# Two streams of matmuls on TensorE keep the order in which they are written; block sums one half product earlier, attention's stages at a higher priority

## The chip, the cores and the metric

The kernel runs on one core of one Trainium2 chip. The metric is the device time of one execution in microseconds (us); three runs of the kernel before gave a median of 1011.45 us. The engines are named as in the profile: PE is TensorE (matmuls), PEld its weight load, DVE is VectorE, ACT is ScalarE, POOL is GpSimd, and SP is SyncE, which issues all DMAs here.

## What is computed

One decoder layer on 256 tokens of width 2048, in fp32. All projections of `x` come first, then three branches (block attention, a gated spatial mix, attention into 256 memory tokens), each multiplied by a SiLU gate, projected to the model's width, weighted with a sigmoid gate, summed, projected once more and normalised:

```python
proj = x @ w_in
q_a, k_a, v_a, z_a, u_g, v_g, z_g, q_c, z_c, g_logit = split(proj)
y_a = _moba_attention(q_a, k_a, v_a) * silu(z_a)            # branch 0, 8 heads
y_g = _spatial_gating(u_g, v_g, w_s, b_s, ...) * silu(z_g)  # branch 1
mem_k, mem_v = mem @ w_mem_k, mem @ w_mem_v
y_c = _memory_attention(q_c, mem_k, mem_v) * silu(z_c)      # branch 2, 4 heads
gates = sigmoid(g_logit)                                    # (b, s, 3, d)
merged = (gates[:, :, 0] * (y_a @ w_branch_attn) + gates[:, :, 1] * (y_g @ w_branch_sgu)
          + gates[:, :, 2] * (y_c @ w_branch_mem))
x = _layer_norm(DN_ALPHA * x + merged @ w_out, ln_g, ln_b)
```

## The kernel before

Every fp32 product is made from fp32r parts. `split` (lines 58 to 60) copies a weight tile to its rounded part `hi` on ACT and computes the rest `lo = v - hi` on DVE; a product is then three matmuls (hi with x's hi, lo with x's hi, hi with x's lo). So each weight needs an ACT and a DVE operation ahead of its matmuls, and each of these matmuls has 512 columns or fewer.

After the memory projections two streams feed PE.

- **C, the classic stream** (`classic`, 160 half steps): the gates zc, then q of memory attention (qc), three gate tiles za, branch 2, five za, q and k of block attention, three ug, branch 0, five ug, zg with the spatial mix, branch 1. A half step of `channel_tile` is 16 matmuls on `acc` banks (`channels_mm`, lines 187 and 188); one of `gated_branch` is 12 (lines 712 to 714). Its weights come by SP as `raw` (line 122) and are split by `prep_half` into `hi`/`lo`, two half chunks ahead. There are three `acc` banks in PSUM; each step n of a `gated_branch` takes two of them (t = 0 and 1) and gives them back when DVE has multiplied them with the gate (`sg`, line 726).
- **S, the Strassen-like stream** (`s_stream`, 8 units of 7 block products, each in 2 halves: 112 half products of 12 matmuls, lines 386 to 388, tile `sM`). Unit u covers a block of weight columns (three branches' gate logits, v of two branches). `s_prep(s)` loads the x sums (`xf`) of half product s, subtracts weight blocks `b` in place on DVE (line 311: the one for the products M5, M6 and M4 ahead of the split, the one for M3 behind it), splits into `sh`/`sl`, and loads the next blocks (`s_load`). Half product s calls `s_prep(s + 2)` behind its matmuls; `sh` and `sl` share four buffers, so two half products are held at a time. `evacuate` copies or adds the results (k, lines 342 to 346), and `s_finish` stores them.

The driver (lines 775 to 783) emits one C half step, then as many S half products as keep S at 112 per 160 - LEAD - TAIL C steps, with LEAD, TAIL = 2, 14: the first S half products come after two C steps, and S ends 14 C steps before C does. `step` runs what the step before put in `late` (evacuations, stores), and `tick` advances each item in `pending` by one stage: an attention head has three (scores, transposes, values), whose result `put_y` splits into `yhl`, the branch's input.

This emission is not what the engines get. The tile framework's scheduler reorders instructions by its own model of times, taking among those that are ready the one with the best priority, by order of emission. Only what `tc.issue_after` ties stays in order. The instruction lists that each engine executes strictly in order are fixed at that point.

Of the kernel before, what the change touches and what calls it, by code (L numbers as in the profile page):

```python
# [1 line left out]

# [25 lines left out]
def decoder_layer(ctx, tc, xT, memT, x_tok, w_st, w_mv, w_mk, w_zc, w_qc, w_za, w_qk, w_ug, w_zg,  # L28
                  w_br, w_o, w_sT, sgu_bc, ln_g, ln_b, out):
    nc = tc.nc  # L30
# [11 lines left out]
    def w2(name, shape=(P, 512)):  # L42
        return work.tile(list(shape), F32, tag="w2", name=name, bufs=6)
# [27 lines left out]

    def tick():
        for item in list(pending):
            item.pop(0)()
            if not item:
                pending.remove(item)

# [107 lines left out]

    def channels_mm(ps, x, hi, lo, first, last):
        nc.tensor.matmul(ps, hi, x, start=first, stop=False)  # L187
        nc.tensor.matmul(ps[:, S:2 * S], lo, x[:, 0:S], start=False, stop=last)

    def channel_tile(xs, name, fin):  # L190

        ps = new_acc(name)
        for h in range(2):
            hi, lo = c_half()
            for k in range(8):
                c = slice(k * P, (k + 1) * P)
# [100 lines left out]

    B11, B12, B22, B21 = range(4)

    def s_prep(s):  # L300
        u, r = divmod(s, 14)
        if u >= UNITS:
            return
        p, h = divmod(r, 2)
        p = PRODUCTS[p]
        if p in FORM:
            t = wts.tile([P, 4, 2 * P], F32R, tag="xsf", name=f"xf{s}", bufs=3)
            nc.sync.dma_start(t.bitcast(F32), xf_d[FORM[p], h])
            xsf[s] = t
        b = lambda blk: rt[u, blk, h]  # L310
        sub = lambda o, x, y: nc.vector.tensor_tensor(o, x, y, op=ALU.subtract)  # L311
        src = {"M1": B11, "M5": B11, "M6": B11, "M4": B11, "M3": B22, "M7": B12, "M2": B21}[p]
        if p == "M5":
            sub(b(B11), b(B12), b(B11))
        elif p == "M6":
            sub(b(B11), b(B22), b(B11))
        elif p == "M4":
            sub(b(B11), b(B21), b(B11))
        hi = wts.tile([P, 2048], F32R, tag="shl", name=f"sh{s}", bufs=4)
        lo = wts.tile([P, 2048], F32R, tag="shl", name=f"sl{s}", bufs=4)  # L320
        split(hi, lo, b(src))
        shl[s] = (hi, lo)
        if p == "M3":
            sub(b(B12), b(B22), b(B12))
            s_load(u, B21, h)
        elif p == "M7":
            s_load(u + 1, B12, h)
        elif p == "M4":
            s_load(u + 1, B11, h)
        elif p == "M2":  # L330
            s_load(u + 1, B22, h)

    def snap(name):
        return work.tile([P, 512], F32, tag="snap", name=name, bufs=5)

    def s_stream(finish):

        bank, kept = {}, {}

        def keep(name, ps):  # L340
            kept[name] = snap(name)
            nc.scalar.activation(kept[name], ps, AF.Copy)

        def result(u, t, n, ps, name):
            r = kept[name]
            nc.vector.tensor_tensor(r, ps, r, op=ALU.add)
            finish(u, t, n, r)

        def evacuate(u, p):
            if p == "M1":  # L350
                keep(f"k1_{u}", bank["b"])
            elif p == "M5":
                keep(f"k5_{u}", bank["d"])
            elif p == "M6":
                keep(f"k6_{u}", bank["b"])
            elif p == "M3":
                result(u, 0, 1, bank["d"], f"k6_{u}")
            elif p == "M7":
                keep(f"k7_{u}", bank["b"])
                result(u, 1, 1, bank["b"], f"k5_{u}")  # L360
            elif p == "M4":
                result(u, 1, 0, bank["c"], f"k7_{u}")
            else:
                result(u, 0, 0, bank["a"], f"k1_{u}")

        BANK = {"M1": "b", "M6": "b", "M7": "b", "M5": "d", "M3": "d", "M4": "c", "M2": "a"}
        for s in range(14 * UNITS):
            u, r = divmod(s, 14)
            p, h = divmod(r, 2)
            p = PRODUCTS[p]  # L370
            if h == 0 and p in ("M1", "M5", "M4", "M2"):
                bank[BANK[p]] = new_sps(f"s{p}_{u}")
            ps = bank[BANK[p]]
            hi, lo = shl.pop(s)
            for kk in range(4):
                k = 4 * h + kk
                if p in FORM:
                    ah, al = xsf[s][:, kk, 0:P], xsf[s][:, kk, P:2 * P]
                else:
                    k += 0 if p == "M1" else 8  # L380
                    t = P if p == "M4" else 0
                    ah, al = xhl[:, k, t:t + P], xhl[:, k, S + t:S + t + P]
                c = slice(kk * 512, (kk + 1) * 512)
                first = h == 0 and kk == 0 and p in ("M1", "M5", "M4", "M2")
                last = h == 1 and kk == 3
                nc.tensor.matmul(ps, ah, hi[:, c], start=first, stop=False, skip_group_check=True)  # L386
                nc.tensor.matmul(ps, ah, lo[:, c], start=False, stop=False, skip_group_check=True)  # L387
                nc.tensor.matmul(ps, al, hi[:, c], start=False, stop=last, skip_group_check=True)  # L388
            xsf.pop(s, None)
            s_prep(s + 2)  # L390
            if h == 1:
                late.append(lambda u=u, p=p: evacuate(u, p))
            yield
# [303 lines left out]
    def gated_branch(b, order):  # L697
        for n in range(4):
            ps = [new_acc(f"b{b}_{n}{t}") for t in range(2)]
            g, prev = {}, {}  # L700
            for t in range(2):
                g[t] = w2(f"sg{b}{t}{n}")
                nc.sync.dma_start(g[t], gl_d[b, t, n])
                nc.scalar.activation(g[t], g[t], AF.Sigmoid)
            for half in range(4):
                hi, lo = c_half()
                for kk in range(2):
                    k = 2 * half + kk
                    c = slice(kk * 512, (kk + 1) * 512)
                    for t in range(2):  # L710
                        yh, yl = (yhl[b][:, k, o + t * P:o + (t + 1) * P] for o in (0, S))
                        nc.tensor.matmul(ps[t], yh, hi[:, c], start=(k == 0), stop=False)  # L712
                        nc.tensor.matmul(ps[t], yh, lo[:, c], start=False, stop=False)  # L713
                        nc.tensor.matmul(ps[t], yl, hi[:, c], start=False, stop=(k == 7))  # L714
                if half == 3:
                    late.append(lambda n=n, ps=ps, g=g: gated(b, order, n, ps, g))
                elif n == 0:
                    late.append(tick)
                yield
# [196 lines left out]
```

## Time and profile before

| | us |
|---|---|
| median of three runs (lowest, highest) | 1011.45 (1009.95, 1011.49) |
| the profiled execution | 1014.38 |
| its span in the profile | 1012.7 |
| PE busy | 982.4, 97% of the span |
| DVE busy | 820.6, 81% |
| ACT busy | 590.6, 58% |

The page's busy times say how full an engine is over the whole span. Where time can still be taken from PE is read in three other views: the stretches (busy time of each engine and TensorE's granted clock between two times), the list of waits (who ended PE's idle time), and the timelines of single instructions. A tile's name carries its number in the instruction lists below (`sh5_1211` is `sh` of half product 5), while the trace leaves numbers out.

### The profile page before, as it was taken

The page shows a single profiled execution, that of the slowest core. Times are in us where ns is not written, and L with a number is a line of the kernel's source. Part 1 is how long each engine was busy: PE and PEld are TensorE (multiplying, and loading weights), DVE is VectorE, ACT ScalarE, POOL GpSimd, SP SyncE. Part 2 cuts the span into 40 slices and gives each one's busy share as a digit, 9 for nine tenths or more (in the row PEclk, how much of TensorE's full clock was granted, in tenths as well). Part 3 has the DMA queues.
Part 4 walks back from the last instruction along what each step waited for, and adds up shares of the span by engine and source line. Part 5 has one row for each costly group of instructions (what it writes and reads, how often), then busy time and mean ns, then how long its engine had stood idle before and what let it go on. Part 6 is the DMA issues. An engine that isn't in the chain of part 4 may idle for free.

```text
span 1012.7 us, 12913 instructions
## 1 busy us (share of the span) xinstructions
PE 982.4 (97%) x4888; PEld 826.9 (82%) x4888; DVE 820.6 (81%) x800; ACT 590.6 (58%) x646; POOL 12.0 (1%) x17
## 2 busy tenths in 40 slices
PE   9999899999999999999999999979998999999995
PEld 7788788888888788888888888858877888878885
DVE  5865987898779799888979898899979877676657
ACT  5654665565577566556556566867555559554430
POOL 0000000000000000000000000000000010000000
PEclk9999999999999999999999999989999999999998
DMA  8899589738965897598379648937994785778622
GB/s 330 313 387 414 181 304 348 277 132 296 364 223 168 295 382 278 165 362 346 134 271 356 236 139 281 382 106 269 414 366 147 284 286 183 249 259 303 238 84 83
DMA packets 68126, 269.28 MB, mean 266 GB/s; under 512 B 7521, under 2 KB 21601, under 8 KB 45537
## 3 DMA queue, kind: packets, MB, share of 16 engines
q1 hardware_dynamic: 68064, 268.47, 72.2%
q8 instruction: 38, 0.62, 0.2%
q14 instruction: 24, 0.19, 0.0%
HBM read 245.37 MB, written 23.07 MB: 265 GB/s over the span
## 4 chain that ended last, share of the span: by engine, by line
PE 85%; DVE 5%; ACT 4%; DMA 3%; issue 2%; POOL 0%; SPq 0%; DVEq 0%; ACTq 0%
PE sM L386 9%; PE sM L387 9%; PE sM L388 9%; PE b L713 4%; PE b L714 3%; PE b L712 3%; PE zc L187 3%; PE k L187 3%; PE qc L187 3%; PE za L187 3%; PE q L187 3%; PE mk L187 3%; PE o L800 3%; PE o L799 3%; PE o L798 3%; PE mv L423 3%
## 5 line engine op out<-in xcount | busy, mean ns | idle before, releaser
L59 ACT ACTIVATE hi<-raw 128x1024 fp32r<-128x1024 f32 (+1 forms) x218 | 228.3, 1051 | 191.4 <-PE o L800 29.1
L60 DVE TENSOR_TENSOR lo<-raw,hi 128x1024 fp32r<-128x1024 f32 (+1 forms) x218 | 263.1, 1214 | 77.2 <-ACT hi L59 76.4
L60 DVE TENSOR_TENSOR sl<-b,sh 128x2048 fp32r<-128x2048 f32 x112 | 256.3, 2291 | 57.1 <-ACT sh L59 56.7
L59 ACT ACTIVATE sh<-b 128x2048 fp32r<-128x2048 f32 x112 | 214.4, 1915 | 99.6 <-PE sM L387 89.3
L311 DVE TENSOR_TENSOR b<-b,b 128x2048 f32<-128x2048 f32 x64 | 146.3, 2289 | 8.0 <-DMA b<-in_w_st_dram 7.8
L386 PE MATMUL sM<-sh,xf 128*128 128x512 f32 x256 | 101.3, 396 | 6.5 <-ACT sh L59 6.5
L387 PE MATMUL sM<-sl,xf 128*128 128x512 f32 x256 | 100.6, 393 | 2.5 <-DVE sl L60 2.5
L388 PE MATMUL sM<-sh,xf 128*128 128x512 f32 x256 | 100.2, 391 | 0.0
L387 PE MATMUL sM<-sl,xhl 128*128 128x512 f32 x192 | 76.8, 400 | 0.6 <-DVE sl L60 0.6
L386 PE MATMUL sM<-sh,xhl 128*128 128x512 f32 x192 | 77.4, 403 | 0.0
L713 PE MATMUL b<-lo,yhl 128*128 128x512 f32 x192 | 76.1, 397 | 1.2 <-DVE lo L60 1.2
L388 PE MATMUL sM<-sh,xhl 128*128 128x512 f32 x192 | 76.3, 397 | 0.0
L714 PE MATMUL b<-hi,yhl 128*128 128x512 f32 x192 | 74.9, 394 | 0.0
L712 PE MATMUL b<-hi,yhl 128*128 128x512 f32 x192 | 74.0, 398 | 0.9 <-ACT hi L59 0.9
L386 PEld LDWEIGHTS sM<-sh,xf 128*128 128x128 f32 x256 | 48.3, 189 | 18.3 <-ACT sh L59 7.9
L387 PEld LDWEIGHTS sM<-sl,xf 128*128 128x128 f32 x256 | 48.2, 188 | 12.9 <-DVE sl L60 3.2
L388 PEld LDWEIGHTS sM<-sh,xf 128*128 128x128 f32 x256 | 48.1, 188 | 10.3
L187 PE MATMUL ug<-xhl,hi 128*128 128x512 f32 x128 | 46.3, 400 | 1.5 <-ACT hi L59 1.5
L187 PE MATMUL q<-xhl,hi 128*128 128x512 f32 x128 | 46.5, 399 | 0.0
L187 PE MATMUL qc<-xhl,hi 128*128 128x512 f32 x128 | 46.2, 400 | 0.0
L187 PE MATMUL zc<-xhl,hi 128*128 128x512 f32 x128 | 45.7, 398 | 0.4 <-ACT hi L59 0.4
L187 PE MATMUL k<-xhl,hi 128*128 128x512 f32 x128 | 46.0, 397 | 0.0
(296 smaller groups left out, 1853.1 us busy)
## 6 DMA issues: line engine op xcount, KB each, us to landing
b<-in_w_st_dram SPq DMA_DIRECT2D x64, 1024.0 KB, 7.2
xf<-xf SPq DMA_DIRECT2D x64, 512.0 KB, 6.0
raw<-in_w_br_dram SPq DMA_DIRECT2D x24, 1024.0 KB, 6.8
raw<-in_w_qk_dram SPq DMA_DIRECT2D x16, 1024.0 KB, 7.3
raw<-in_w_o_dram SPq DMA_DIRECT2D x16, 1024.0 KB, 5.4
raw<-in_w_mk_dram SPq DMA_DIRECT2D x8, 1024.0 KB, 10.1
raw<-in_w_zc_dram SPq DMA_DIRECT2D x8, 1024.0 KB, 6.5
raw<-in_w_qc_dram SPq DMA_DIRECT2D x8, 1024.0 KB, 7.6
```

The costliest lines, as they stand in the source:

```text
L59: nc.scalar.activation(hi, v, AF.Copy)
L60: nc.vector.tensor_tensor(lo, v, hi.bitcast(F32), op=ALU.subtract)
L187: nc.tensor.matmul(ps, hi, x, start=first, stop=False)
L311: sub = lambda o, x, y: nc.vector.tensor_tensor(o, x, y, op=ALU.subtract)
L386: nc.tensor.matmul(ps, ah, hi[:, c], start=first, stop=False, skip_group_check=True)
L387: nc.tensor.matmul(ps, ah, lo[:, c], start=False, stop=False, skip_group_check=True)
L388: nc.tensor.matmul(ps, al, hi[:, c], start=False, stop=last, skip_group_check=True)
L423: nc.tensor.matmul(ps[t][n], lhs, rhs[:, n * 512:(n + 1) * 512], start=(k == 0 and rhs is hi and lhs is xh[t]), stop=(k == KT - 1 and lhs ...
L712: nc.tensor.matmul(ps[t], yh, hi[:, c], start=(k == 0), stop=False)
L713: nc.tensor.matmul(ps[t], yh, lo[:, c], start=False, stop=False)
L714: nc.tensor.matmul(ps[t], yl, hi[:, c], start=False, stop=(k == 7))
L798: nc.tensor.matmul(ps[:, 0:n], mh, hi, start=first, stop=False)
```

## The change

Four things are changed.

1. `in_turn` ties each piece of matmuls to the last matmul of the previous half step, whichever stream that was of: on PE, C half steps and S half products stay in the order in which the driver emits them. Inside an S half product or a gated half step the order stays free.
2. The block sums for M5, M6 and M4 leave `s_prep` for `s_sum`, which half product s calls as `s_sum(s + 3)` just ahead of `s_prep(s + 2)`: these 48 sums are emitted one half product before the split that reads them. The 16 for M3 stay in `s_prep`.
3. `tick` runs its stages under a higher priority for the scheduler.
4. LEAD, TAIL become 5, 11: S begins three C steps later and ends three later; the ratio stays 112 to 144.

```diff
+    behind = [None]
+    def in_turn():
+        return tc.issue_after(behind[0].ins) if behind[0] is not None else nullcontext()
@@ def tick():
-            item.pop(0)()
+            with tc.high_priority(100):
+                item.pop(0)()
@@ def channel_tile(xs, name, fin):
+            with in_turn():
+                for k in range(8):
+                    c = slice(k * P, (k + 1) * P)
+                    mm = channels_mm(ps, xs(8 * h + k), ...)
+            behind[0] = mm
@@
+    def s_sum(s):
+        u, r = divmod(s, 14)
+        if u >= UNITS:
+            return
+        p, h = divmod(r, 2)
+        other = {"M5": B12, "M6": B22, "M4": B21}.get(PRODUCTS[p])
+        if other is not None:
+            o = rt[u, B11, h]
+            nc.vector.tensor_tensor(o, rt[u, other, h], o, op=ALU.subtract)
@@ def s_prep(s):
-        if p == "M5":
-            sub(b(B11), b(B12), b(B11))
-        elif p == "M6":
-            sub(b(B11), b(B22), b(B11))
-        elif p == "M4":
-            sub(b(B11), b(B21), b(B11))
@@ s_stream: for s in range(14 * UNITS): for kk in range(4):
-                nc.tensor.matmul(ps, ah, hi[:, c], ...)      # and two more
+                with in_turn():
+                    nc.tensor.matmul(ps, ah, hi[:, c], ...)  # and two more, the last is mm
+            behind[0] = mm
             xsf.pop(s, None)
+            s_sum(s + 3)
             s_prep(s + 2)
@@ after the memory projections
     s_prep(1)
+    s_sum(2)
@@ gated_branch: for kk in range(2): for t in range(2):
+                        with in_turn():                      # the three matmuls, the last is mm
+                behind[0] = mm
@@
-    LEAD, TAIL = 2, 14
+    LEAD, TAIL = 5, 11
```

In the changed file the lines above move: `channels_mm` is at 194 and 195, the S matmuls at 401 to 403, the branch's at 731 to 733, the gate's multiplication at 746, the block sums at 318 (`s_sum`) and 331 (M3).

**Place 1, where the S stream begins.** On PE, around the end of gate tile zc0. Before:

```order
L187 MATMUL zc0_993<-xhl_96,hi16_1_890 128x512
L188 MATMUL zc0_993<-xhl_96,lo16_1_891 128x256
L386 MATMUL sM1_0_1063<-sh0_917,xhl_96 128x512
L387 MATMUL sM1_0_1063<-sl0_918,xhl_96 128x512
L388 MATMUL sM1_0_1063<-sh0_917,xhl_96 128x512
...
L386 MATMUL sM1_0_1063<-sh1_921,xhl_96 128x512
L386 MATMUL sM5_0_1154<-sh2_1079,xf2_1076 128x512
L387 MATMUL sM1_0_1063<-sl1_922,xhl_96 128x512
...
L187 MATMUL zc1_1037<-xhl_96,hi17_0_994 128x512
L386 MATMUL sM5_0_1154<-sh3_1121,xf3_1118 128x512
```

Half products 0, 1 and 2 of S (sh0 to sh2) stand between zc0 and zc1 here. After the change:

```order
L194 MATMUL zc0_994<-xhl_96,hi16_1_890 128x512
L195 MATMUL zc0_994<-xhl_96,lo16_1_891 128x256
L194 MATMUL zc1_1038<-xhl_96,hi17_0_995 128x512
L195 MATMUL zc1_1038<-xhl_96,lo17_0_996 128x256
...
L194 MATMUL zc1_1038<-xhl_96,hi17_1_1016 128x512
L195 MATMUL zc1_1038<-xhl_96,lo17_1_1017 128x256
...
L194 MATMUL zc2_1087<-xhl_96,hi18_0_1039 128x512
L195 MATMUL zc2_1087<-xhl_96,lo18_0_1040 128x256
...
L401 MATMUL sM1_0_1136<-sh0_917,xhl_96 128x512
L402 MATMUL sM1_0_1136<-sl0_918,xhl_96 128x512
```

Now zc1 and zc2 follow zc0, and half product 0 comes behind zc2. On DVE in the same stretch, before:

```order
L208 TENSOR_TENSOR zc0_1058<-zc0_993,zc0l_1059 128x256
L311 TENSOR_TENSOR b1_0_0_551<-b2_0_0_777,b1_0_0_551 128x2048
L60 TENSOR_TENSOR sl1_922<-b0_0_1_833,sh1_921 128x2048
L60 TENSOR_TENSOR sl2_1080<-b0_0_0_775,sh2_1079 128x2048
L311 TENSOR_TENSOR b0_0_1_833<-b1_0_1_608,b0_0_1_833 128x2048
L311 TENSOR_TENSOR b0_0_0_775<-b2_0_0_777,b0_0_0_775 128x2048
L60 TENSOR_TENSOR lo17_0_995<-raw17_841,hi17_0_994 128x1024
L60 TENSOR_TENSOR lo17_1_1016<-raw17_841,hi17_1_1015 128x1024
```

Here sl2 and two block sums stand between sl1 and lo17_0, the first `lo` of zc1. After the change:

```order
L217 TENSOR_TENSOR zc0_1059<-zc0_994,zc0l_1060 128x256
L331 TENSOR_TENSOR b1_0_0_551<-b2_0_0_777,b1_0_0_551 128x2048
L60 TENSOR_TENSOR sl1_922<-b0_0_1_833,sh1_921 128x2048
L318 TENSOR_TENSOR b0_0_1_833<-b1_0_1_608,b0_0_1_833 128x2048
L331 TENSOR_TENSOR b1_0_1_608<-b2_0_1_835,b1_0_1_608 128x2048
L60 TENSOR_TENSOR lo17_0_996<-raw17_841,hi17_0_995 128x1024
L60 TENSOR_TENSOR lo17_1_1017<-raw17_841,hi17_1_1016 128x1024
L60 TENSOR_TENSOR lo18_0_1040<-raw18_894,hi18_0_1039 128x1024
```

The split for half product 2 (sl2) and its next sum have left, and the sums of the second half (b0_0_1 and b1_0_1) stand ahead of lo17_0.

**Place 2, the step from n = 1 to n = 2 of branch 2.** On PE (b2_10 and b2_11 are the two banks of n = 1, b2_20 and b2_21 those of n = 2). Before:

```order
L712 MATMUL b2_10_2808<-hi38_1_2836,yhl2_1609 128x512
L712 MATMUL b2_11_2809<-hi38_1_2836,yhl2_1609 128x512
L712 MATMUL b2_20_2954<-hi39_0_2875,yhl2_1609 128x512
L387 MATMUL sM1_2_2673<-sl33_2803,xf33_2799 128x512
L388 MATMUL sM1_2_2673<-sh33_2802,xf33_2799 128x512
L386 MATMUL sM1_2_2673<-sh33_2802,xf33_2799 128x512
```

The matmuls of n = 1, of n = 2 and of half product 33 are mixed here. After the change:

```order
L732 MATMUL b2_11_2750<-lo38_1_2795,yhl2_1573 128x512
L733 MATMUL b2_11_2750<-hi38_1_2794,yhl2_1573 128x512
L731 MATMUL b2_20_2888<-hi39_0_2834,yhl2_1573 128x512
L732 MATMUL b2_20_2888<-lo39_0_2835,yhl2_1573 128x512
...
L731 MATMUL b2_21_2889<-hi39_0_2834,yhl2_1573 128x512
L732 MATMUL b2_21_2889<-lo39_0_2835,yhl2_1573 128x512
```

Now n = 2 starts right behind n = 1 without any of S between. On DVE, before:

```order
L60 TENSOR_TENSOR sl33_2803<-b0_2_1_2361,sh33_2802 128x2048
L60 TENSOR_TENSOR lo38_1_2837<-raw38_2698,hi38_1_2836 128x1024
L60 TENSOR_TENSOR lo39_0_2876<-raw39_2773,hi39_0_2875 128x1024
L60 TENSOR_TENSOR sl34_2869<-b2_2_0_2418,sh34_2868 128x2048
L60 TENSOR_TENSOR lo39_1_2913<-raw39_2773,hi39_1_2912 128x1024
L726 TENSOR_TENSOR sg201_2810<-b2_10_2808,sg201_2810 128x512
L60 TENSOR_TENSOR sl35_2906<-b2_2_1_2511,sh35_2905 128x2048
L726 TENSOR_TENSOR sg211_2813<-b2_11_2809,sg211_2813 128x512
```

Here sg201, which gives the first bank back, stands behind splits alone. After the change:

```order
L318 TENSOR_TENSOR b0_2_0_2399<-b2_2_0_2515,b0_2_0_2399 128x2048
L60 TENSOR_TENSOR lo39_0_2835<-raw39_2712,hi39_0_2834 128x1024
L318 TENSOR_TENSOR b0_2_1_2471<-b2_2_1_2594,b0_2_1_2471 128x2048
L60 TENSOR_TENSOR lo39_1_2869<-raw39_2712,hi39_1_2868 128x1024
L60 TENSOR_TENSOR sl32_2831<-b0_2_0_2399,sh32_2830 128x2048
L746 TENSOR_TENSOR sg201_2751<-b2_10_2749,sg201_2751 128x512
L746 TENSOR_TENSOR sg211_2754<-b2_11_2750,sg211_2754 128x512
```

Two block sums (L318), two `lo` and sl32 now stand directly ahead of sg201.

**Place 3, the end of n = 0 of branch 0, DVE.** The eighth attention head's result o7 becomes sza7 and then the last part of `yhl0`. Before:

```order
L608 TENSOR_TENSOR sza7_5203<-o7_5374,sza7_5203 128x256
L60 TENSOR_TENSOR sl85_5639<-b0_6_1_5462,sh85_5638 128x2048
L311 TENSOR_TENSOR b1_6_0_5292<-b2_6_0_5501,b1_6_0_5292 128x2048
L60 TENSOR_TENSOR sl86_5721<-b0_6_0_5425,sh86_5720 128x2048
L311 TENSOR_TENSOR b0_6_1_5462<-b1_6_1_5367,b0_6_1_5462 128x2048
L636 BN_STATS vst_5662<-vg_5405 128x6
L60 TENSOR_TENSOR yhl0_3644<-sza7_5203,yhl0_3644 128x256
L311 TENSOR_TENSOR b0_6_0_5425<-b2_6_0_5501,b0_6_0_5425 128x2048
L311 TENSOR_TENSOR b1_6_1_5367<-b2_6_1_5569,b1_6_1_5367 128x2048
L640 BN_AGGR vmv_5663<-vst_5662 128x2
L726 TENSOR_TENSOR sg000_5382<-b0_00_5380,sg000_5382 128x512
L726 TENSOR_TENSOR sg010_5385<-b0_01_5381,sg010_5385 128x512
```

Splits and sums of half products 85 and 86 stand between sza7 and yhl0 here, S being well ahead of the driver's order. After the change:

```order
L626 TENSOR_TENSOR sza7_5162<-o7_5332,sza7_5162 128x256
L60 TENSOR_TENSOR lo69_1_5441<-raw69_5288,hi69_1_5440 128x1024
L360 TENSOR_TENSOR k6_5_5362<-sM5_5_5116,k6_5_5362 128x512
L60 TENSOR_TENSOR sl79_5435<-b1_5_1_4631,sh79_5434 128x2048
L60 TENSOR_TENSOR yhl0_3575<-sza7_5162,yhl0_3575 128x256
L654 BN_STATS vst_5731<-vg_5459 128x6
L746 TENSOR_TENSOR sg000_5340<-b0_00_5338,sg000_5340 128x512
L746 TENSOR_TENSOR sg010_5343<-b0_01_5339,sg010_5343 128x512
```

Now lo69_1, the evacuation of half product 77 (into k6) and sl79 stand between them.

## Rows read from the trace of the kernel before

**Rows 1.** The page, engines: busy us, share of the span, instructions.

```profile
PE 982.4 (97%) x4888; PEld 826.9 (82%) x4888; DVE 820.6 (81%) x800; ACT 590.6 (58%) x646; POOL 12.0 (1%) x17
```

**Rows 2.** Stretches: start:end, length, busy us of five engines, TensorE clock, DMA share, GB/s.

```profile
100.00:125.00 25.00, 21.71 (x101) 17.54 (x100) 23.36 (x15) 14.83 (x14) 0.00 (x0) 0.93 0.58 201
400.00:500.00 100.00, 100.00 (x517) 84.80 (x516) 88.07 (x71) 60.00 (x66) 0.00 (x0) 1.00 0.70 256
650.00:700.00 50.00, 44.80 (x176) 35.16 (x175) 45.17 (x42) 37.54 (x40) 0.00 (x0) 0.90 0.55 203
740.00:790.00 50.00, 44.17 (x224) 36.35 (x223) 46.49 (x41) 29.14 (x30) 3.45 (x1) 1.00 0.63 232
```

**Rows 3.** Who PE waited for: us in total, times, longest.

```profile
PE sM L386 <- ACT sh L59: 6.5, 3, 2.8
PE sM L387 <- DVE sl L60: 3.1, 3, 1.8
PE mix L668 <- POOL ws L657: 1.8, 1, 1.8
```

**Rows 4.** Three stretches with a lower clock, columns as in rows 2.

```profile
106.30:112.40 6.10, 3.26 (x9) 2.49 (x9) 5.58 (x4) 4.82 (x5) 0.00 (x0) 0.72 0.48 187
667.70:672.20 4.50, 4.49 (x13) 3.57 (x14) 4.50 (x3) 2.20 (x3) 0.00 (x0) 0.62 0.00 0
679.00:685.80 6.80, 6.61 (x15) 4.86 (x16) 6.80 (x7) 1.50 (x3) 0.00 (x0) 0.51 0.00 0
```

**Rows 5.** Timeline of PE at the lower clock: start, us, line, tiles.

```profile
671.39 0.63 PE L387 MATMUL sM<-sl,xhl 128*128 128x512 f32 x1
671.82 0.50 PE L388 MATMUL sM<-sh,xhl 128*128 128x512 f32 x1
```

**Rows 6.** Timeline of PE where the S stream begins.

```profile
103.31 0.39 PE L386 MATMUL sM<-sh,xhl 128*128 128x512 f32 x1
103.54 0.39 PE L387 MATMUL sM<-sl,xhl 128*128 128x512 f32 x1
...
109.28 0.80 PE L386 MATMUL sM<-sh,xf 128*128 128x512 f32 x1 [2.84 <-ACT sh L59]
```

**Rows 7.** Timeline of ACT in the same stretch.

```profile
103.79 1.91 ACT L59 ACTIVATE sh<-b 128x2048 fp32r<-128x2048 f32 x1
...
107.02 0.42 ACT L491 ACTIVATE zc<-zc 128x256 f32<-128x256 f32 x1
...
109.14 1.99 ACT L59 ACTIVATE hi<-raw 128x1024 fp32r<-128x1024 f32 x2
```

**Rows 8.** Tile raw, issues from 98 to 104 us: durations, starts, landing.

```profile
L122 SPq DMA_DIRECT2D raw<-in_w_zc_dram x2: 333/356/378, 98.9 to 103.9; - x2
...
DMA to landing us min/median/max: 8.2/8.6/9.1
```

**Rows 9.** Timeline of DVE in the same stretch.

```profile
104.27 2.28 DVE L311 TENSOR_TENSOR b<-b,b 128x2048 f32<-128x2048 f32 x1
106.47 2.28 DVE L60 TENSOR_TENSOR sl<-b,sh 128x2048 fp32r<-128x2048 f32 x1
...
115.88 2.36 DVE L60 TENSOR_TENSOR lo<-raw,hi 128x1024 fp32r<-128x1024 f32 x2
```

**Rows 10.** Timeline of DVE, two short operations.

```profile
661.88 0.69 DVE L346 TENSOR_TENSOR k<-sM,k 128x512 f32<-128x512 f32 x1
...
674.42 0.41 DVE L60 TENSOR_TENSOR yhl<-sza,yhl 128x256 fp32r<-128x256 f32 x1
```

**Rows 11.** The page, groups: count, busy, mean ns, idle before and releaser.

```profile
L311 DVE TENSOR_TENSOR b<-b,b 128x2048 f32<-128x2048 f32 x64 | 146.3, 2289 | 8.0 <-DMA b<-in_w_st_dram 7.8
```

**Rows 12.** Tile ptT: count, ns least/median/most, first and last start.

```profile
L599 ACT ACTIVATE ptT<-pt x8: 473/492/494, 477.4 to 659.5; 128x384 f32<-128x384 f32 x8
```

**Rows 13.** Timeline of SP's DMA issues near the end.

```profile
869.40 0.38 SPq L403 DMA_DIRECT2D gl<-k  x1
...
877.05 1.48 SPq L703 DMA_DIRECT2D sg<-gl  x2
```

More of the change, by code (lines that the diff above doesn't have):

```diff
@@ L1 @@
-from contextlib import ExitStack
+from contextlib import ExitStack, nullcontext
 import concourse.bass as bass
@@ L187, in channels_mm @@
         nc.tensor.matmul(ps, hi, x, start=first, stop=False)
-        nc.tensor.matmul(ps[:, S:2 * S], lo, x[:, 0:S], start=False, stop=last)
+        return nc.tensor.matmul(ps[:, S:2 * S], lo, x[:, 0:S], start=False, stop=last)
     def channel_tile(xs, name, fin):
@@ L194, in channel_tile @@
             hi, lo = c_half()
-            for k in range(8):
-                c = slice(k * P, (k + 1) * P)
-                channels_mm(ps, xs(8 * h + k), hi[:, c], lo[:, c], h == 0 and k == 0, h == 1 and k == 7)
+            with in_turn():
+                for k in range(8):
+                    c = slice(k * P, (k + 1) * P)
+                    mm = channels_mm(ps, xs(8 * h + k), hi[:, c], lo[:, c], h == 0 and k == 0, h == 1 and k == 7)
+            behind[0] = mm
             if h == 1:
@@ L385, in s_stream @@
                 last = h == 1 and kk == 3
-                nc.tensor.matmul(ps, ah, hi[:, c], start=first, stop=False, skip_group_check=True)
-                nc.tensor.matmul(ps, ah, lo[:, c], start=False, stop=False, skip_group_check=True)
-                nc.tensor.matmul(ps, al, hi[:, c], start=False, stop=last, skip_group_check=True)
+                with in_turn():
+                    nc.tensor.matmul(ps, ah, hi[:, c], start=first, stop=False, skip_group_check=True)
+                    nc.tensor.matmul(ps, ah, lo[:, c], start=False, stop=False, skip_group_check=True)
+                    mm = nc.tensor.matmul(ps, al, hi[:, c], start=False, stop=last, skip_group_check=True)
+            behind[0] = mm
             xsf.pop(s, None)
+            s_sum(s + 3)
             s_prep(s + 2)
@@ L711, in gated_branch @@
                         yh, yl = (yhl[b][:, k, o + t * P:o + (t + 1) * P] for o in (0, S))
-                        nc.tensor.matmul(ps[t], yh, hi[:, c], start=(k == 0), stop=False)
-                        nc.tensor.matmul(ps[t], yh, lo[:, c], start=False, stop=False)
-                        nc.tensor.matmul(ps[t], yl, hi[:, c], start=False, stop=(k == 7))
+                        with in_turn():
+                            nc.tensor.matmul(ps[t], yh, hi[:, c], start=(k == 0), stop=False)
+                            nc.tensor.matmul(ps[t], yh, lo[:, c], start=False, stop=False)
+                            mm = nc.tensor.matmul(ps[t], yl, hi[:, c], start=False, stop=(k == 7))
+                behind[0] = mm
                 if half == 3:
```

## Prediction

> **What bounds the kernel now.** I read the page's engine totals first: PE is busy for 982.4 us, 97% of the span, and DVE for 820.6 [rows 1], so the end is set by PE's matmuls and by what PE waits for. The stretches say where it waits [rows 2]: from 400 to 500 us PE has no idle time at all, with DVE at 88%; from 100 to 125 it idles 25.00 - 21.71 = 3.29 us, from 650 to 700 5.20, from 740 to 790 5.83, together 14.3 us. The list of waits says on whom [rows 3]: 6.5 us in three waits of S matmuls for `sh`, 3.1 in three for `sl`, 1.8 in one of the spatial mix for POOL. So it is S that waits for its own weights, and the instruction lists show why: between sza7 and yhl0 (place 3) DVE splits half products 85 and 86, where the changed list has 79. S ran in a burst, faster than ACT and DVE can split for it, and it let C's weights lie ready.
>
> A wait costs more than its idle time. An S matmul is listed at 0.39 us, yet the next starts 0.23 us after it [rows 6]: a pipeline that runs dry loses 0.39 - 0.23 = 0.16 us. The list counts seven [rows 3], and 14.3 - 11.4 = 2.9 us are left for smaller ones; I take ten, 1.6 us. And behind the longer waits TensorE was granted its lower level (1.2 GHz) for a while: after the wait of 2.84 us at 109.28 [rows 6] and in two later stretches the mean clock was 0.72, 0.62 and 0.51 [rows 4]. At a mean of 0.62 over 4.5 us, (1 - 0.62) / 0.5 x 4.5 = 3.4 us lay at half clock; the others give 3.4 and 6.7. There matmuls start 0.43 us apart [rows 5] instead of 0.23, a loss of 1 - 0.23 / 0.43 = 46% of that time: 1.6, 3.1 and, in the first stretch, of which the wait itself is a part, 1.5. That is 6.2 us. All losses before: 14.3 + 1.6 + 6.2 = **22.1 us**. I sum against the profiled execution, 1014.38 us with a span of 1012.7; it lies 2.93 above the median of 1011.45, and I take the same 2.93 off at the end.
>
> **The change part by part.** Matmuls, splits and sums are the same in number, so every term is a wait. `in_turn` ties PE to PE, whose list is in order anyway: nothing waits for the tie itself; it costs the scheduler's freedom to put ready work into a gap. The three stretches of before lose their cause (no bursts, the sum no longer in the chain from a freed buffer to `sl`): all of the 22.1 us is given back. Against it stand the places that the instruction lists of the changed kernel show.
>
> (1) Place 1. PE goes from zc0, whose end is where S begins today (103.31 [rows 6]), straight to zc1, which needs raw17. That chunk is issued at 98.9 and lands at most 9.1 us later, at 108.0 [rows 8]. ACT is free by then: the SiLU of zc0 ends at 107.02 + 0.42 = 107.44, and hi17_0 takes 1.99 / 2 = 1.00 us [rows 7], so it is there at 109.1. DVE is the last one. Block operations follow each other at 106.47 - 104.27 = 2.20 us [rows 9]; as today the first sum stands at 104.27 and sl1 at 106.47, then come the two new ones at 108.67 and 110.87, then lo17_0 at 113.07, which takes 2.36 us for two, some 1.14 for the first [rows 9]: 114.2. PE loses 114.2 - 103.31 - 0.23 = 10.7 us, all of it on the path, for half products 0 to 2 that filled this gap are now behind zc2. The lower clock behind it costs between 1.5 and 3.1 (above); after a wait four times the longest so far I take the upper end. **13.8 us** (12.2 to 13.8). What is late next: raw18 is issued by 103.9 [rows 8] and lands by 113, before its turn.
>
> (2) Place 2, and the eight transitions like it in three branches. The second bank of step n + 1 is the first one of step n, free when the latter's multiplication (sg201) has run. Between sg200 and sg201 the changed DVE list has seven block operations, four `lo` and the two multiplications: 7 x 2.20 + 4 x 1.14 + 2 x 0.61 = 21.2 us, the multiplication taken from another 512-column operation of DVE, 0.69 less 0.08 of overlap [rows 10]. PE has 96 matmuls and the first six of b2_20, 102 x 0.23 = 23.5. So DVE keeps up by 2.3 us unless it is in a block operation when it should begin; the wait is 0 to 2.2 us. Over nine transitions I take 2.5 us in all (0 to 6.6, a third of nine times 2.2). The trace has three `acc` banks and PE at 100.00 of 100 us between 400 and 500 [rows 2], but only the gates and block attention run there, the first ptT at 477.4 [rows 12]. The Trainium skill (Perfetto Trace Analysis, Optimizing Tensor Performance, Matmuls) says that independent groups should rotate through PSUM banks so that one's evacuation overlaps the next one's matmuls; by that rule alone, three banks rotating, this term would be 0 and the sum 2.5 us lower, which no row here decides.
>
> (3) Place 3. The last part of `yhl` waits on DVE for the evacuation of half product 77, so for its last matmul: then 0.61 (as k, 0.69 [rows 10]), sl79 2.20 and yhl 0.33 (0.41 less the overlap [rows 10]), 3.1 us in all, against ten matmuls that PE still has, 2.3. PE waits 0.8 us, or up to 3.0 with one block operation more ahead. I take 2.0, since lo69_1 and the signals between the engines come on top, and half of a lower clock's 3.1 (the wait of 1.8 for POOL [rows 3] left the clock of its stretch at 1.00 [rows 2], that of 2.84 [rows 6] didn't): **3.5 us** (0.8 to 6.1).
>
> (4) Attention's stages come earlier, and head 2's values stand right behind its transposes on PE. The copy ptT takes 0.49 us [rows 12] and has one `hi` of 1.00 ahead [rows 7]: 0.5 to 1.5, I take **1.3 us**.
>
> (5) S in step with C: from the release of its buffers half product s + 2 needs `sh` 1.91 [rows 7] and `sl` 2.20, with a `lo` 1.14, a sum 2.20 (2.289 with its overlap [rows 11]) and an evacuation 0.61 between, 8.06 us. PE has one half product and some two half steps of C, 36 x 0.23 = 8.3. That is even: 0 most of the time, as between 400 and 500 [rows 2], up to 0.9 where a second evacuation stands ahead. Around units 5 and 6, where the norm of v adds to DVE, I take four at 0.8: **3.2 us** (0 to 4.5).
>
> (6) LEAD, TAIL. S ends three half steps later, so the last gate logits are stored later, and branch 1's step n = 2 loads them. Today 877.05 - 869.40 = 7.65 us lie between store and load on SP [rows 13]; three half steps are 36 x 0.23 = 8.3 us. 0 if it fits, 7.65 if all of it shows; I take **0.5**, since it fits with 0.6 to spare.
>
> `high_priority` and `s_sum` issue nothing of their own, and no DMA is added; SP's loads are moved with their half products past stores that wait for evacuations, 0 as long as they land in 8.2 to 9.1 us [rows 8].
>
> Sum after: 13.8 + 2.5 + 3.5 + 1.3 + 3.2 + 0.5 = 24.8 us, against 22.1: +2.7. 1014.38 + 2.7 - 2.93 = 1014.15, **1014.2 us**. The bounds go far: the low ends give 12.2 + 0 + 0.8 + 0.5 + 0 + 0 = 13.5, 8.6 us faster, 1002.9; the high ones 13.8 + 6.6 + 6.1 + 1.5 + 4.5 + 7.65 = 40.2, but not all at once.
>
> **The rivals.** *The order is as good as it looks* (faster). One mechanism: DVE is not in a block operation when a bank or a `yhl` is due, so transitions, place 3 and S's steps show next to nothing, and only (1), (4) and 1 us remain: 16.1 us, 6.0 less than before, 1005.4. It decides once (2), (3), (5) and (6), 9.7 us in my sum, together stay under 22.1 - 2.0 - 15.1 = 5.0 us. For it: 100 us without idle time at DVE's 88% [rows 2]. Against it: that stretch has no branch step and no burst either.
>
> *A wash*: these four come to between 5.0 and 9.0 us, and the result lies within 2.0 us of 1011.45.
>
> *The tail shows* (slower): the store and load of (6) are not hidden and sit ahead of a branch's splits on ACT: 7.2 us more than I took, 1021.4.
>
> *Every transition waits* (slower): sg2n1 and its like come a whole block operation late nine times, 9 x 2.2 = 19.8 us in place of 2.5: +17.3, 1031.5. Against it: DVE has room in its 88% with the same splits and sums [rows 2]. The Trainium skill (Perfetto Trace Analysis, Optimization Strategy) states that one gap repeating on the engine that should be saturated can mean too little SBUF or PSUM for the next tile; by that rule the three `acc` banks would be this gap. No run so far shows it.
>
> That the change doesn't do what it says is out: the lists show C and S alternating.
>
> **How the numbers follow.** The forecast, slower by more than 0.2% (2.0 us, about what a measurement of this kernel can tell from no change) but under 1020: 0.36. The wash: 0.30. Faster: 0.26. The tail 0.04, the transitions 0.04. So faster 0.26, same 0.30, slower 0.44. The likeliest case alone spans 1013.5 to 1020. The range must take in most of the faster case and the tail: 1003.5 to 1021.5, leaving out the transitions and the edges of both sides.
>
> **What would show it.** In the changed profile: one PE wait of some 10 us near 104, put down to `lo` on DVE, with a lower clock behind it (without it the sum is wrong by 13.8 us, and the change is faster); no idle time left at 650 to 700 and 740 to 790 of the kind `sM` on `sh`; waits of branch matmuls at line 731 on the gate's multiplication, 0 to 2.2 us each; one at 733 on `yhl` of 1 to 3 us; small waits of line 402 on `sl`. The forecast is wrong if the waits of S on `sh` and `sl` stay at 9.6 us, or if (2) is zero nine times.

## The result and the profile after

The changed kernel takes 1017.95 us (median of four runs, 1016.46 to 1020.71) against 1011.47 (1009.95 to 1011.71): a ratio of 1.0071, 95% interval 1.0049 to 1.0092. It is slower by 6.5 us. The profiled execution took 1017.01 us with a span of 1015.3.

The page's engine line and the list of PE's waits answer to [rows 1] and [rows 3]. The page gives busy us, share of the span and instructions for each engine:

```profile
PE 979.2 (96%) x4888; PEld 824.2 (81%) x4888; DVE 819.7 (81%) x800; ACT 586.9 (58%) x642; POOL 17.3 (2%) x17
```

The list gives who PE waited for, us in total, times and the longest:

```profile
PE zc L194 <- ACT hi L59: 5.4, 1, 5.4
PE zc L195 <- DVE lo L60: 4.9, 1, 4.9
PE b L731 <- DVE sg L746: 4.3, 3, 1.8
PE b L733 <- DVE yhl L60: 2.6, 1, 2.6
PE b L731 <- ACT yhl L59: 1.8, 1, 1.8
...
PE o L622 <- ACT ptT L617: 1.1, 1, 1.1
...
PE sM L402 <- DVE sl L60: 0.9, 2, 0.5
```

No S matmul waits for `sh` any more, and those for `sl` come to 0.9 us in place of 3.1. But the chain of C has taken over: zc1 waits twice, 10.3 us together, branch matmuls wait 4.3 us for banks (sg), 4.4 us for `yhl`. The stretches of [rows 2] but the one from 400 to 500 (start:end, length, busy us of PE, PEld, DVE, ACT and POOL, granted clock, DMA share, GB/s), and one more with the lower clock at place 1:

```profile
100.00:125.00 25.00, 14.68 (x70) 12.06 (x69) 17.56 (x12) 10.28 (x11) 0.00 (x0) 0.80 0.58 210
650.00:700.00 50.00, 45.62 (x195) 37.06 (x194) 42.51 (x38) 37.45 (x37) 0.00 (x0) 0.97 0.96 363
740.00:790.00 50.00, 50.00 (x258) 42.17 (x257) 44.59 (x45) 31.85 (x33) 1.12 (x2) 1.00 0.96 382
107.70:117.90 10.20, 4.93 (x14) 3.85 (x15) 8.21 (x6) 2.31 (x3) 0.00 (x0) 0.50 0.26 81
```

From 740 to 790 PE is now full, where it idled 5.83 us. From 650 to 700 the idle time is 4.4 us in place of 5.2, of another kind, and from 100 to 125 it is 10.3 in place of 3.29; from 107.7, at the end of the first of the two waits, the clock was at half for 10.2 us.

Place 1, on the timelines of PE, ACT and DVE (start, us, line, tiles; idle time before and what ended it in brackets). They answer to [rows 6], [rows 7] and [rows 9]:

```profile
108.06 0.80 PE L194 MATMUL zc<-xhl,hi 128*128 128x512 f32 x1 [5.42 <-ACT hi L59]
113.76 0.58 PE L195 MATMUL zc<-xhl,lo 128*128 128x256 f32 x1 [4.91 <-DVE lo L60]
```

```profile
106.95 2.00 ACT L59 ACTIVATE hi<-raw 128x1024 fp32r<-128x1024 f32 x2 [0.36 <-DMA raw<-in_w_zc_dram]
```

```profile
107.95 2.29 DVE L318 TENSOR_TENSOR b<-b,b 128x2048 f32<-128x2048 f32 x1
110.28 2.29 DVE L331 TENSOR_TENSOR b<-b,b 128x2048 f32<-128x2048 f32 x1
112.49 3.49 DVE L60 TENSOR_TENSOR lo<-raw,hi 128x1024 fp32r<-128x1024 f32 x3
```

The first wait ends when raw17 has landed and ACT has made hi17_0 (the first of the two copies from 106.95); the second lasts until DVE has been through the two sums that stand ahead of lo17_0 (L318 at 107.95, L331 at 110.28) and through lo17_0 itself.

At the first transition of branch 2, DVE and then PE:

```profile
322.67 2.28 DVE L331 TENSOR_TENSOR b<-b,b 128x2048 f32<-128x2048 f32 x1
324.88 1.22 DVE L60 TENSOR_TENSOR lo<-raw,hi 128x1024 fp32r<-128x1024 f32 x1
326.01 1.28 DVE L746 TENSOR_TENSOR sg<-b,sg 128x512 f32<-128x512 f32 x2
```

```profile
326.75 0.50 PE L731 MATMUL b<-hi,yhl 128*128 128x512 f32 x1 [1.75 <-DVE sg L746]
```

DVE goes from an M3 sum (L331) to a `lo` to the gate's two multiplications (L746) without a gap, and reaches these at 326.01, when PE has been through its six matmuls on the third bank. The bank is free when the first of the two is done, and PE goes on at 326.75. At the next transition, DVE and then PE:

```profile
347.16 1.28 DVE L746 TENSOR_TENSOR sg<-b,sg 128x512 f32<-128x512 f32 x2
347.90 0.50 PE L731 MATMUL b<-hi,yhl 128*128 128x512 f32 x1 [1.82 <-DVE sg L746]
```

From one pair of multiplications to the next DVE takes 347.16 - 326.01 = 21.15 us. PE has 84 matmuls between the two places where it needs a bank, starts on them at 326.75 and stands still from 347.90 - 1.82 = 346.08: 19.3 us. The difference is the wait.

At place 3:

```profile
657.82 0.68 DVE L360 TENSOR_TENSOR k<-sM,k 128x512 f32<-128x512 f32 x1
658.42 2.28 DVE L60 TENSOR_TENSOR sl<-b,sh 128x2048 fp32r<-128x2048 f32 x1
660.62 0.41 DVE L60 TENSOR_TENSOR yhl<-sza,yhl 128x256 fp32r<-128x256 f32 x1
```

```profile
661.09 1.22 PE L733 MATMUL b<-hi,yhl 128*128 128x512 f32 x2 [2.62 <-DVE yhl L60]
```

Evacuation, sl79, `yhl`, and PE is released: the chain of the prediction, link by link.

To compare places I added up, over all matmul starts of PE, what each step to the next start takes beyond 0.2285, 0.118 and 0.109 us (the usual steps behind 512, 256 and 128 columns). This holds waits and lower clock together, in us, for two profiles of either kernel (the second ones come from the experiments):

| stretch | before, 1st | before, 2nd | after, 1st | after, 2nd |
|---|---|---|---|---|
| whole span | 46.4 | 45.5 | 49.0 | 54.6 |
| place 1 (100 to 133) | 5.5 | 6.1 | 13.3 | 13.2 |
| branch 2 (318 to 376) | 0.3 | -0.4 | 4.8 | 7.7 |
| place 3 (645 to 672) | 5.5 | 5.5 | 6.5 | 6.8 |
| rest of branch 0 (672 to 712) | 5.9 | 5.0 | 0.1 | 0.0 |
| 712 to 900 | 9.3 | 9.1 | 3.3 | 4.5 |

### The profile page after: what moved, and what is told of

Its sections match the earlier page's. It is cut to its first block, busy times and chain, and to the rows that moved or that the text cites. A ratio compares the mean times of both kernels' runs of the same rounds, so it can differ in the third digit from the quotient of the medians.

```text
span 1015.3 us, 12897 instructions
## 1 busy us (share of the span) xinstructions
PE 979.2 (96%) x4888; PEld 824.2 (81%) x4888; DVE 819.7 (81%) x800; ACT 586.9 (58%) x642; POOL 17.3 (2%) x17
## 4 chain that ended last, share of the span: by engine, by line
PE 81%; DVE 8%; DMA 5%; issue 3%; ACT 2%; SPq 0%; DVEq 0%; ACTq 0%
PE sM L401 9%; PE sM L402 9%; PE sM L403 9%; PE qc L194 3%; PE za L194 3%; PE q L194 3%; PE zg L194 3%; PE o L820 3%; PE o L819 3%; PE o L818 3%; PE k L194 3%; PE b L733 3%; PE zc L194 3%; PE b L731 3%; PE ug L194 3%
## 5 line engine op out<-in xcount | busy, mean ns | idle before, releaser
L318 DVE TENSOR_TENSOR b<-b,b 128x2048 f32<-128x2048 f32 x48 | 109.6, 2283 | 9.2 <-DMA b<-in_w_st_dram 9.0
L401 PE MATMUL sM<-sh,xhl 128*128 128x512 f32 x192 | 75.8, 395 | 0.0
L403 PE MATMUL sM<-sh,xhl 128*128 128x512 f32 x192 | 75.3, 392 | 0.0
L731 PEld LDWEIGHTS b<-hi,yhl 128*128 128x128 f32 x192 | 36.0, 188 | 15.5 <-DVE sg L746 6.0
L194 PE MATMUL zg<-xhl,hi 128*128 128x512 f32 x128 | 45.8, 397 | 0.0
```

What stands on the lines that cost most here:

```text
L318: nc.vector.tensor_tensor(o, rt[u, other, h], o, op=ALU.subtract)
L403: mm = nc.tensor.matmul(ps, al, hi[:, c], start=False, stop=last, skip_group_check=True)
```

## The experiments

My first theory was the prediction's: the tie (`in_turn`) makes both the gain (S no longer runs ahead) and the loss (place 1 above all), so that filling place 1 with half products gives its 13 us back. Its rivals: the time is paid elsewhere; the earlier sums, the priority or LEAD do the harm. Each ratio below is to the kernel before, run beside it, with its 95% interval.

**b_again** is the kernel before, unchanged.

> The kernel before, unchanged, to see how far one profile of it stands for its other executions. Theory (the execution that I summed against carried lower-clock time that the others don't have, so that taking 2.93 us off the changed kernel as well was wrong): ratio 1.000, and the new profile's execution lies within 1.5 us of the median of 1011.5, with less than 3 us lost at the lower clock behind the waits of 650 to 690 us, where I counted 4.7. Rival (every profiled execution is about 3 us longer than a plain one): the profile shows about 1014.4 us again.

Ratio 1.0008 (0.9996 to 1.0019). The profiled execution took 1013.53 us, 2.0 above the 1011.5 that I had named, and there was one stretch of 3.4 us less at the lower clock than in [rows 4]:

```profile
667.60:671.00 3.40, 3.04 (x7) 2.46 (x8) 3.40 (x2) 2.53 (x4) 0.00 (x0) 0.50 0.00 0
681.30:684.70 3.40, 3.40 (x10) 2.66 (x9) 3.40 (x3) 1.06 (x1) 0.00 (x0) 0.50 0.00 0
```

At 46% that is 6.8 x 0.46 = 3.1 us, a little over what I expected, so neither side was quite right. But 17 runs of the kernel before that were timed beside it go from 1010.05 to 1014.73 with a median of 1011.95: 1014.38 was an execution from the upper end, and 2.93 us were its own. Nor do other kernels show an offset of profiled executions: that of the changed kernel (1017.01) and that of no_turn (999.90) lie below their medians.

**no_turn** takes the tie out of the changed kernel:

```diff
 def in_turn():
-    return tc.issue_after(behind[0].ins) if behind[0] is not None else nullcontext()
+    return nullcontext()
```

> The changed kernel without the tie between C and S: the scheduler orders PE freely again; sums, priority and LEAD, TAIL as changed. Theory (the order on PE makes both the gain and the loss): PE starts as before with half products 0 to 2 behind zc0, place 1 costs under 4 us, S runs in bursts again and waits for sh and sl for over 6 us; 1008 to 1013 us. Rival (the earlier sums or the priority lengthen DVE's way to lo and sg, whatever the order on PE): 1016 to 1020.

1001.02 us, ratio 0.9895 (0.9881 to 0.9910): 11 us faster than before and 17 faster than the changed kernel, beyond what my theory allowed. Waits of PE:

```profile
PE sM L401 <- ACT sh L59: 3.1, 2, 2.8
PE sM L402 <- DVE sl L60: 2.4, 3, 1.8
```

So the tie alone costs 17 us. It does take away more of S's waits (0.9 us are left with it, 5.5 without, where I expected over 6, and 9.6 before), but the other parts of the change gain without it. By the measure of the table above, 8.0 of the 17 us lie at place 1, 4.1 in branch 2, 2.8 at place 3 and 2.2 from 712 to 900. The lists of DVE, ACT and SP change with the tie too, so this is its price together with what the scheduler then makes of them.

**lead2** sets LEAD, TAIL back in the changed kernel:

```diff
-    LEAD, TAIL = 5, 11
+    LEAD, TAIL = 2, 14
```

> The changed kernel with LEAD, TAIL = 2, 14 as before. Here half product 0 stands behind the first half step of zc1, but zc1 still follows zc0 directly on PE, and on DVE the same two block operations stand ahead of lo17_0. Theory (the tie makes place 1, not LEAD): the wait of some 10 us at zc1 stays; 1015 to 1019 us. Rival (place 1 comes from S beginning three C steps later): the wait falls under 4 us and the time to 1004 to 1008.

1022.34 us, ratio 1.0096 (1.0081 to 1.0112). The two waits of zc1 are there as before:

```profile
PE zc L194 <- ACT hi L59: 5.7, 1, 5.7
PE zc L195 <- DVE lo L60: 4.7, 1, 4.7
PE b L731 <- ACT yhl L59: 3.6, 1, 3.6
PE b L731 <- DVE sg L746: 3.6, 1, 3.6
PE mix L686 <- POOL ws L675: 2.8, 1, 2.8
```

Place 1 belongs to the tie, not to LEAD. The time lies above my 1015 to 1019. By the table's measure 12.2 us are lost behind 672 us, where the changed kernel loses 3.4: the wait of 3.6 for sg stands in branch 0 here, and the mix waits 2.8. Branch 2, without a wait for a bank, loses 3.8 less.

**lead_only** and **prio_only** are the kernel before with one part each:

```diff
-    LEAD, TAIL = 2, 14
+    LEAD, TAIL = 5, 11
```

> The kernel before with LEAD, TAIL = 5, 11 and nothing else. Theory (without the tie the gain of 11 us comes from S being emitted three C steps later: it then runs less far ahead, half product 80 instead of 84 beside o7 on PE): most of the gain, 1002 to 1006 us, the waits of sM on sh and sl near 650 to 700 and 740 to 760 fall from 9.6 us to under 6. Rival (the gain comes from attention's stages having priority): 1009 to 1013.

```diff
 for item in list(pending):
-    item.pop(0)()
+    with tc.high_priority(100):
+        item.pop(0)()
```

> The kernel before with the higher priority for the stages of tick and nothing else. Theory (LEAD makes the gain): 1008 to 1012 us. Rival (priority makes it, sza7 and yhl coming earlier, so that C has work and S stops running ahead; half product 81 instead of 84 beside o7 on PE): 1001 to 1006.

lead_only 1004.82 us, 0.9938 (0.9915 to 0.9960); prio_only 1009.80, 0.9974 (0.9963 to 0.9986). LEAD gives 6 to 7 us and the priority 2 to 3; together with the sums, in no_turn, it is 11. Waits of lead_only:

```profile
PE sM L386 <- ACT sh L59: 5.2, 3, 2.8
PE sM L387 <- DVE sl L60: 3.5, 2, 2.6
```

The detail of my theory for lead_only isn't borne out: its waits for `sh` and `sl` were to fall under 6 us and are 8.7 in this profile, whose execution (1010.94 us) was the slowest of its eight. In prio_only they come to 8.3. The time is settled, the way it is saved in this kernel isn't.

The fourth part needs no run. The instruction lists of all five engines are the same, in the same order, whether the 48 sums are emitted at their old place or one half product ahead, in the kernel before as in the changed one: `s_sum` moves nothing. The lists of no_turn are those of the kernel before with LEAD and priority alone.

With this the tie can be priced twice: prio_only to lead2 is +12.5 us, no_turn to the changed kernel +17.

**first3** fills place 1 in the changed kernel:

```diff
-    while done_s < S_STEPS and done_s * (C_STEPS - LEAD - TAIL) < (done_c - LEAD) * S_STEPS:
+    while done_s < S_STEPS and (done_s < 3 and done_c >= 2
+                                or done_s * (C_STEPS - LEAD - TAIL) < (done_c - LEAD) * S_STEPS):
```

> The changed kernel, but the driver emits half products 0, 1 and 2 right behind zc0, so that they stand between zc0 and zc1 on PE again, as before; all else stays. Theory (place 1 is lost on the path: 10.3 us of waiting and about 2.5 at the lower clock): the waits of zc1 for hi17_0 and lo17_0 fall from 10.3 us to under 2, and the time from 1017.95 by 11 to 13 us to 1005 to 1007, ratio to before 0.994 to 0.996. Rival (the gap at place 1 is slack that S pays for elsewhere: whoever starts S earlier waits for its blocks or for C later): under 4 us gained, 1014 or more.

1028.09 us, ratio 1.0155 (1.0137 to 1.0173): 10 us slower than the changed kernel, where I expected 11 to 13 faster. The theory fell, and the rival's mechanism came out larger than its own words:

```profile
PE b L731 <- DVE sg L746: 6.7, 3, 4.0
PE mix L686 <- POOL ws L675: 5.9, 1, 5.9
PE sM L402 <- DVE sl L60: 4.0, 2, 2.4
PE zc L195 <- DVE lo L60: 2.4, 4, 1.0
```

Place 1 did shrink: in place of 10.3 us PE waits 2.4 us for sl1 (at 108.69) and 2.4 for `lo`. But the lists of DVE, ACT and SP moved as well, far behind the place that was edited. A bank of branch 0 comes 4.0 us late at 703, and the mix now waits 5.9 us at 823 for POOL's select on `ws`, which took 9.71 us. The timeline of POOL, and the busy times meanwhile (columns as above):

```profile
813.04 9.71 POOL L675 TENSOR_SCALAR_AFFINE_SELECT ws<-ws 128x128 f32<-128x128 f32 x1 [19.16 <-DMA ws<-in_w_sT_dram]
```

```profile
813.00:823.00 10.00, 4.11 (x24) 3.33 (x23) 9.61 (x10) 3.46 (x3) 9.71 (x1) 0.80 0.26 76
```

**sums_behind** changes one thing in the changed kernel: each block sum is queued on DVE behind the last `lo` of C that was emitted before it, so that at place 1 lo17_0 follows sl1 directly.

```diff
 def split(hi, lo, v): ...
-    nc.vector.tensor_tensor(lo, v, hi.bitcast(F32), op=ALU.subtract)
+    return nc.vector.tensor_tensor(lo, v, hi.bitcast(F32), op=ALU.subtract)
@@ prep_half
-    split(hi[:, c:c + n], lo[:, c:c + n], ...)
+    lo_last[0] = split(hi[:, c:c + n], lo[:, c:c + n], ...)
@@ s_sum, and the M3 sum of s_prep
+    with tc.issue_after(lo_last[0].ins):
         nc.vector.tensor_tensor(o, rt[u, other, h], o, op=ALU.subtract)
```

> The changed kernel, with each block sum queued on DVE behind the last lo of C that was emitted before it: at place 1 lo17_0 now follows sl1 directly. Theory (4.9 us of place 1 are the two sums ahead of lo17_0): the wait of zc1 for hi17_0 stays at 5 to 6 us, the one for lo17_0 falls from 4.9 to about 1.1, and the time by 3 to 5 us to 1013 to 1015. Rival (as where S began earlier, the other lists move with it, and a tied PE can't step aside): no gain, 1016 to 1024.

1006.03 us, ratio 0.9934 (0.9916 to 0.9952): 12 us faster than the changed kernel, more than twice what I expected, and faster than the one before. Its waits, and DVE at place 1:

```profile
PE zc L194 <- ACT hi L59: 5.4, 1, 5.4
PE b L733 <- DVE sg L748: 4.5, 3, 2.5
PE sM L404 <- DVE sl L60: 2.4, 1, 2.4
...
PE zc L195 <- DVE lo L60: 0.5, 1, 0.5
```

```profile
106.21 2.29 DVE L60 TENSOR_TENSOR sl<-b,sh 128x2048 fp32r<-128x2048 f32 x1 [1.37 <-ACT sh L59]
109.33 2.36 DVE L60 TENSOR_TENSOR lo<-raw,hi 128x1024 fp32r<-128x1024 f32 x2 [0.83 <-ACT hi L59]
```

The first wait of zc1 stays at 5.4 us and the second falls from 4.9 to 0.5, as the theory says. The rest of the gain is at place 3: no wait for `yhl` is left there, and the stretch from 645 to 672 loses 1.5 us in place of 6.5. By the same measure place 1 loses 8.2 in place of 13.3; the two profiled executions differ by 9.8 us. In DVE's list `yhl` now stands ahead of lo69_1, the evacuation and sl79. The waits for sg stay (4.5 us).

**first3_behind** adds the half products of first3 to that:

> The changed kernel with both: the block sums behind C's splits, and half products 0 to 2 between zc0 and zc1. Theory (half products 0 to 2 cover the landing of raw17, which is the 5.4 us that is left at place 1, but half product 2 then waits some 2.5 to 3 us for sh2 and sl2, as in the kernel before): the wait for hi17_0 falls from 5.4 to under 1, the gain against the sums alone (1006.0) is 2 to 4 us, 1002 to 1004, with no mix wait over 2 us. Rival (starting S early is what hurts the later stages, by the mix for POOL and sg at 703): 1008 to 1016, with these waits back.

1004.44 us, ratio 0.9923 (0.9904 to 0.9942):

```profile
PE sM L404 <- DVE sl L60: 4.5, 3, 2.4
PE b L733 <- DVE sg L748: 2.0, 3, 0.8
...
PE zc L195 <- DVE lo L60: 1.5, 3, 1.1
```

The wait for hi17_0 is gone, no mix wait is left, and the span of the profile is 5.6 us shorter than that of sums_behind. The time lies just above my 1002 to 1004. In the times the gain of 1.6 us is within what two intervals overlap, so it isn't established. It does show that starting S early was not what hurt first3; the lists that came with it were.

**nt_behind** is no_turn with the sums behind C's splits (both diffs above).

> The changed kernel without the tie of PE, and with the block sums behind the C splits as above: a candidate for the best version. Theory (with PE free, DVE's order costs little: what is late is stepped round): within 4 us of 1001.0, that is 998 to 1005. Rival (the sums then come too late for S, whose splits wait for them): 1006 to 1012, with waits of sM on sl over 6 us.

996.25 us (995.16 to 997.09), ratio 0.9836 (0.9818 to 0.9854): the best version found, 15 us faster than the kernel before. It lies below my 998 to 1005: the sums' place is worth about 5 us with a free PE too.

```profile
PE sM L403 <- ACT sh L59: 2.8, 1, 2.8
...
PE sM L404 <- DVE sl L60: 1.4, 3, 0.9
```

**after_again** is the changed kernel once more.

> The changed kernel, unchanged, with a second profile. Theory (its places are fixed by the instruction lists, the spread lies in the lower clock behind them): the waits of zc1 come to 10 to 11 us again, those of branch matmuls on sg, yhl and ACT to 8 to 9, median 1017 to 1019. Rival (the waits vary from execution to execution with the landing of the loads): one of these sums moves by over 2 us.

1018.85 us, ratio 1.0071 (1.0053 to 1.0089), the same as at first. Its profiled execution took 1022.59 us, 5.6 more than the first:

```profile
PE b L731 <- DVE sg L746: 5.6, 3, 3.0
PE zc L194 <- ACT hi L59: 5.3, 1, 5.3
PE zc L195 <- DVE lo L60: 5.0, 1, 5.0
PE b L733 <- DVE yhl L60: 2.2, 1, 2.2
```

Place 1 repeats to 0.1 us. The branch matmuls wait 9.6 us in all, above my 8 to 9 (8.7 at first): those for sg went from 4.3 to 5.6 us, the longest from 1.8 to 3.0. There was more time at the lower clock as well, a stretch at 351 us and twice as long a one at 662. So the theory holds for place 1. By the table's measure 2.9 of the 5.6 us lie in branch 2, 1.2 from 712 to 900, where the mix waits 1.0 for POOL, and 1.1 before 100 us, which the places don't explain.

## Why the prediction was right, and where not

The forecast was slower, at 1014.2 us with 1003.5 to 1021.5; it is 1017.95. By its own steps:

- **Place 1** was 13.8 us (12.2 to 13.8), with DVE as the last one: 13.3 and 13.2 in two profiles. Its lo17_0 was to be there at 114.2, that is 10.7 us of loss. In place of one wait for `lo` two came, for hi17_0 and for lo17_0, 10.33 us together, and PE went on at 113.76. That DVE is the last one holds: in sums_behind, without the two sums ahead of lo17_0, only the first wait is left, for the landing of raw17.
- **The transitions** (2) were mis-sized: 2.5 us, measured 4.8 and 7.7, all in branch 2, and none in the other two branches. I had taken that DVE keeps up by 2.3 us and misses only when it happens to be in a block operation. Its 21.2 us from sg200 to sg201 were right (21.15). PE's 23.5 us were not: I counted 102 matmuls from the end of n = 0, as if sg200 ran at that moment, but at 320 to 327 us DVE works without a gap from one block operation to the next, M3's sum among them, and from bank to bank PE has only 84 matmuls, 19.3 us. So DVE arrives late as a rule there, by 1.75, 1.82 and 0.73 us. With three of nine transitions waiting, the rival with all nine did not come either. The rule on rotating PSUM banks that I set against this term (the Trainium skill, Perfetto Trace Analysis, Optimizing Tensor Performance, Matmuls) did not make it zero: three banks rotate here, and PE still waited 4.3 to 5.6 us.
- **Place 3** (3) was 3.5 us with the right chain; 6.5 and 6.8 were lost, as a wait of 1.8 us for ACT's half of `yhl` came ahead of it, which I hadn't listed, and the clock fell each time.
- **Head 2** (4): 1.3 us, and a wait of 1.1 came. **S in step with C** (5): 3.2 us, but only 0.9 of waits. **The tail** (6): 0.5 us, and no wait is listed.
- **What is given back.** Of the 9.6 us of S's waits 0.9 were left, but only in part for the reasons that I gave. The tie takes 4.6 of them (5.5 are left in no_turn); the earlier sums moved nothing in any list. And the tie isn't needed for a gain: by the table's measure no_turn loses 31.9 us, 14.5 less than before, without it. I had costed the tie as the loss of the scheduler's freedom and then looked for that loss only where the new lists showed a gap; as an edit by itself it is worth 12 to 17 us.
- **From the profile to the median.** My sum said +2.7 us between the profiled executions, and 1017.01 - 1014.38 is +2.6. This is partly luck, since a second pair of profiles differs by 9.1 (1022.59 - 1013.53). In the first pair, too, errors cancel: the places came to 13.3 + 4.8 + 6.5 + 1.1 + 0.9 = 26.6 us, not 24.8, and as the whole rose by only 2.6 (46.4 to 49.0 in the table), 24.0 were given back, not 22.1. What failed is taking off the 2.93 us by which one profiled execution of the kernel before exceeded its median, from a kernel whose executions needn't share it: without that step the forecast is 1017.1.

Two things stay open. LEAD's 6 to 7 us are measured, but the one profile of lead_only, of its longest execution, doesn't show where they come from. And that a change at place 1 moves lists 600 us later, for the worse, in first3, and that ties on the sums alone put `yhl` ahead of sl79 at place 3 in sums_behind (they are on all 64 sums, not on those of place 1 alone), is seen in the lists; why the scheduler chose so wasn't tested.

## What to carry to other kernels

Fixing the order on one engine doesn't fix what feeds it: PE's list was tied, DVE's was still the scheduler's choice, with two sums ahead of the `lo` that PE was to wait for. A scheduler that is free to order PE's list puts other matmuls into such a gap; a tied list stands still. So tie the producer's list first (12 us in sums_behind, and about 5 in nt_behind, where PE's list is free) and look there before tying the consumer. And when a change has several parts, price each alone: here one part gained 6 to 7 us, one 2 to 3, one nothing, and the fourth lost 12 to 17.

## What the runs showed of the hardware

The same select of 128 x 128 elements on POOL took from 0.29 to 9.71 us within one execution of first3. During the longest one DVE was busy for 9.61 of 10 us, with sums and splits that read two tiles, and PE stood still for 5.9 us because of it. The Trainium skill (GPSIMD Engine Reference, 1. Specifications) says that POOL shares its SBUF interfaces with VectorE, with contention where a DVE instruction has two SBUF inputs; this agrees with the row, though no run here took DVE's work away beside it. The twelve profiles of this case say more than one row: the 11 selects with no DVE operation beside them all took 0.29 to 0.30 us, and each of the 67 that took 0.5 us or more ran beside a DVE that paused for at most 0.16 us meanwhile. Mix waits of 1.0 to 5.9 us on POOL came and went between the kernels, without any edit to the mix.

The length of one wait of PE doesn't tell whether its clock falls. In after_again the wait of 3.04 us that ends at 329.03 left the granted clock at 1.00 (2.4 GHz) from 329 to 333, while behind one of 1.81 us that ends at 350.18 it was at 0.50 (1.2 GHz) from 351.2 to 354.6. In the prediction I had gone by the length, for place 3.
